# A hybrid mLSTM and DeltaNet block on one core: the DeltaNet output in normal seven-product order throughout, and the mLSTM output's last 512 columns behind it

## The chip, the cores and the metric

The kernel runs on one core of a Trainium2 chip (trn2). The metric is the device time of one execution in microseconds (us). The median of three runs before the change is 2251.95 us (2249.82 to 2252.3).

## The reference

One layer takes x, 512 tokens by 2048 channels, in float32. An input projection feeds two token mixers, an mLSTM and a gated DeltaNet, and two sets of merge gates. Each mixer ends in 512 tokens by 2048 channels, h_a and h_b. What follows is the part that the change touches, cut to its core:

```python
y_a = jnp.matmul(h_a, w_out[:2048])       # mLSTM output, 2048 columns
y_b = jnp.matmul(h_b, w_out[2048:])       # DeltaNet output, 2048 columns
y = sigmoid(gate_a) * y_a + sigmoid(gate_b) * y_b
h = x + y
return h * rsqrt(mean(h * h, axis=-1) + 1e-6) * final_norm_w
```

The last line needs the sum of squares over all 2048 columns of a token before any column of that token can be stored.

## The kernel before, in words

**Number format.** TensorE multiplies float32 by three matmuls of a shorter format: every operand is a high part and a low part, and high times high, high times low and low times high are added in PSUM. A weight tile of 128 by 512 is loaded by the SP queue (L180, L183), ScalarE casts it to the high part `wh` (L136), and VectorE subtracts to get the low part `wl` (L139). The activations are held as `uh` and `ul`, 16 tiles of 128 channels by 512 tokens. All tokens stay on the chip and are cut into four token tiles of 128, so a weight tile of a plain product serves 4 x 3 = 12 matmuls.

**Buffers.** Four buffers of one kind (tag `wr`, NRAW = 4) are shared by the plain weights, by reloaded activations and by gate tiles `ty`; the seven-product part has a second kind (tag `wr3`), three buffers of three tiles.

**Output stage, mLSTM.** The columns 0 to 1023 of y_a are made earlier, in four narrow blocks. At 1965.74 us of the profiled execution two wide blocks begin, columns 1024 to 1535 and 1536 to 2047, each 16 weight tiles x 12 = 192 matmuls (L1570 to L1572). After each, the gate is applied (a tanh form: gate plus one, times the product, times 0.5), x is added, and the result goes to a scratch array in DRAM, `y_d` (L1556 to L1561). During the second wide block `uh` and `ul` are overwritten tile by tile with the DeltaNet's activations (`load_h`), since nothing reads the mLSTM's any more; those stay in DRAM as `hm_d`.

**Output stage, DeltaNet.** y_b is made in two seven-product blocks, as in Strassen's scheme, of 1024 columns each (`OUTS`). A block has an A-half, 8 quads with 4 products of 6 matmuls (192), and a B-half, 8 quads with 3 products (144). A quad is three 128 x 512 tiles of weights loaded into a `wr3` buffer (L533), summed on VectorE (L556, L557) and split. The A-half leaves a sum `ts` in DRAM (`t2o_d`) for the B-half. Gated results of the first block are added into `y_d` by accumulating DMAs of the POOL queue (L1343), each of which holds a `ty` buffer until it has landed.

**The last block before the change** departs from that order. In its A-half POOL subtracts a second weight tile, `b21` (L519 loads it into a `wr` buffer, L560 subtracts, L561 stores to `t2o_d`). Its B-half is `final_y`: 24 single weight tiles (L1401) in the order m5, m7, m1, six matmuls each (L1413 to L1415). Beside it, `hf` (four token tiles of all 2048 columns) is filled from `y_d` (L1435), ScalarE squares (L1431), POOL multiplies by the final norm's weights (`weigh`, L1442), and the factor of a token tile is made at L1447 to L1449. Token tiles 2 and 3 are done ahead of the end; tiles 0 and 1 end behind the last matmuls, and stores go out on SP (L1464).

**What sets the order.** TensorE's instructions stand in the order in which the code is written. On the other engines a scheduler orders by dependence and by priorities (`urgent` ahead, `behind` later). A tick-driven list of generators (`start`, `tick`) sets when loads and side work are issued. `plan`, `limit` and `prepare` say how far ahead plain weights are loaded (4) and split (3). A DMA queue is in order: an issue that waits for a buffer holds up all that stand behind it.

Of the kernel before, what the change touches and what calls it, by code (L numbers as in the profile page):

```python
# [15 lines left out]
P = 128  # L16
# [40 lines left out]
def hybrid_body(  # L57
# [101 lines left out]
    plan += [("o", nb * NO, k) for nb in range(YNARROW * NB // NO, D // NO) for k in range(KT)]  # L159
# [340 lines left out]
    def seven_stage(sbp, su, s4, X, t2_d, w_, k0, blocks, sinks, hook, final=None):  # L500
# [5 lines left out]
                 for g in ("A" if final and b == len(blocks) - 1 else "AB") for i in range(KH)]  # L506
        rawq, partq, b21 = [], {}, {}

        def in_final(b):
            return final is not None and b == len(blocks) - 1  # L510

        def load_b21(q):

            if q < len(quads) and in_final(quads[q][3]):
                _, c1, c2, b, g, i = quads[q]
                k2 = slice((k0 + 2 * i + 1) * P, (k0 + 2 * i + 2) * P)
                with tc.high_priority(offset=2 * PRIO):
                    b21[q] = wp.tile([P, NO], F32, tag="wr", name="b21", bufs=NRAW)
                    nc.sync.dma_start(b21[q], w_[k2, c1:c1 + NO])  # L519
# [25 lines left out]
        def prep_sums(q):  # L545
# [49 lines left out]
        def seven(n0, kind, c1, c2):  # L595
# [5 lines left out]
            if in_final(n0 // (2 * KH)):  # L601
                fin = final(c1, c2, m1, m5, m7, LHS["B"], split, t2_d[(n0 // (2 * KH)) % 2])
# [14 lines left out]
            if in_final(n0 // (2 * KH)):  # L617
                for n in range(KH - 2):
                    prep_sums(n0 + n + 1)
                    prep_pair(n0 + n + 1)  # L620
                    load_quad()
                    for m in range(4):
                        if n == KH - 3 and m == 2:
                            prep_sums(n0 + KH - 1)
                            prep_pair(n0 + KH - 1)
                        product(n, m)
                for m in range(4):
                    for n in (KH - 2, KH - 1):
                        fin(2 * m + n - KH + 2)
                        product(n, m)  # L630
                fin(8)
                return
            N = 2 * KH
            for n in range(N - 2):
                if n == N - 3 and n0 + N + 1 < len(quads) and in_final(quads[n0 + N][3]):
                    load_b21(n0 + N)
# [137 lines left out]
    def begin_mixers():  # L774

        limit[0] = len(plan)
        prepare(nfront - 1)
# [550 lines left out]
    ssf, rf = bia[:, 0:3 * NC].rearrange("p (c n) -> p c n", c=NC), bia[:, 3 * NC:4 * NC]  # L1328

    def sink_y(c1, c2, m1, m5, m7, last):  # L1330

        tgs = {}
        U1, C22 = ([X2[:, q, t, :] for t in range(2)] for q in range(2))

        def load(key, c, col):
            t = tgs[key] = wp.tile([P, NO], F32, tag="wr", name="ty", bufs=NRAW)
            nc.sync.dma_start(t, tg_d[c, :, D + col:D + col + NO])

        def put(key, ps, c, col, now=True):
            t = tgs[key]  # L1340
            with urgent(3) if now else behind("V"):
                V.scalar_tensor_tensor(out=t, in0=t, scalar=1.0, in1=ps, op0=ALU.add, op1=ALU.mult)
            G.dma_start(y_d[c, :, col:col + NO], t, accum_op=ALU.add)  # L1343

        def late_(n, c, col, x_):
            load(n, c, col)
# [3 lines left out]
        def half_b():  # L1350

            for t in range(2):
                load((22, t), 2 + t, c2)
            for t in range(2):
                load((11, t), t, c1)
# [5 lines left out]
            for t in range(2):  # L1361
                load((12, t), t, c2)
# [10 lines left out]
        if not last:  # L1373
            start(half_b(), 4 * KH + 2)
        return (lambda t: put((11, t), m1[t], t, c1)), end5, end7

    def final_y(c1, c2, m1, m5, m7, lhs, split, t4_d):

        U1, C22 = ([X2[:, q, t, :] for t in range(2)] for q in range(2))
        pieces = [(m, i) for m in (1, 2, 0) for i in range(KH)]  # L1380
        ps = (m1, m5, m7)
        rawp, partp = [], []
        hf, fw, jk, ty = {}, {}, {}, {}


        def load_gates():
            order = ((2, c2), (3, c2), (0, c2), (1, c2), (2, c1), (3, c1), (0, c1), (1, c1))
            for n, (c, col) in enumerate(order):
                if n % 3 == 0:
                    t = late["sb"].tile([P, 3, NO], F32, tag="wr3", name="ty", bufs=3)  # L1390
                o = ty[c, col] = t[:, n % 3, :]
                nc.sync.dma_start(o, tg_d[c, :, D + col:D + col + NO])
                yield 1

        def load():
            if len(rawp) < len(pieces):
                m, i = pieces[len(rawp)]
                k2 = slice((KT + 2 * i + 1) * P, (KT + 2 * i + 2) * P)
                with tc.high_priority(offset=2 * PRIO):
                    r = wp.tile([P, 1, NO], F32, tag="wr", name="wr", bufs=NRAW)  # L1400
                    newest["S"] = nc.sync.dma_start(r[:, 0, :], (w_out[k2, c1:c1 + NO], w_out[k2, c2:c2 + NO], t4_d[i])[m]).ins  # L1401
                rawp.append(r)

        def prep():
            if len(partp) < len(pieces):
                with tc.high_priority(offset=2 * PRIO):
                    partp.append(split(rawp[len(partp)], False)[0])

        def part(j, t):
            m, i = pieces[j]  # L1410
            hi, lo = partp[j]
            ah, al = lhs[m](i, slice(t * P, (t + 1) * P))
            T.matmul(ps[m][t], ah, hi, start=False, stop=False, skip_group_check=True)  # L1413
            T.matmul(ps[m][t], ah, lo, start=False, stop=False, skip_group_check=True)  # L1414
            T.matmul(ps[m][t], al, hi, start=False, stop=(i == KH - 1), skip_group_check=True)  # L1415

        def times(c, col, src, tie=True):
            t = ty[c, col]
            with behind("V") if tie else urgent(3):
                V.scalar_tensor_tensor(out=t, in0=t, scalar=1.0, in1=src, op0=ALU.add, op1=ALU.mult)  # L1420

        def plus(c, col, eng, tie=True):
            o = hf[0][:, c, col:col + NO]
            with ExitStack() as e:
                if eng is V:
                    e.enter_context(behind("V") if tie else urgent(3))
                eng.tensor_tensor(out=o, in0=o, in1=ty[c, col], op=ALU.add)  # L1427

        def square(c, a, b, n, tie=True):
            with behind("A") if tie else urgent(3):  # L1430
                A.activation(jk[0][:, 0:b - a], hf[0][:, c, a:b], AF.Square, accum_out=ssf[:, c, n:n + 1])  # L1431

        def known(c, a, b):
            with behind("S"):
                nc.sync.dma_start(hf[0][:, c, a:b], y_d[c, :, a:b])  # L1435

        def weight(a, b):
            with behind("S"):
                nc.sync.dma_start(fw[0][:, a:b], final_norm_w[a:b].partition_broadcast(P))

        def weigh(c, a, b):
            G.tensor_tensor(out=hf[0][:, c, a:b], in0=hf[0][:, c, a:b], in1=fw[0][:, a:b], op=ALU.mult)  # L1442

        def factor(c, tie=True):
            r = rf[:, c:c + 1]
            with behind("V") if tie else urgent(3):
                V.reduce_sum(out=r, in_=ssf[:, c, :], axis=mybir.AxisListType.X)  # L1447
                V.tensor_scalar(out=r, in0=r, scalar1=1.0 / D, scalar2=EPS, op0=ALU.mult, op1=ALU.add)
            G.tensor_tensor(out=r, in0=r, in1=mhalf[:, 0:1], op=ALU.pow)  # L1449

        def by_act(c, a, b, tie=True):
            with behind("A") if tie else urgent(2):
                A.mul(hf[0][:, c, a:b], hf[0][:, c, a:b], rf[:, c:c + 1])

# [171 lines left out]
```

## Time and profile before

| | |
|---|---|
| Runs, median of 3 | 2251.95 us |
| Profiled execution, its own time (span) | 2252.6 us, 0.65 us above the median |
| TensorE busy | 2183.0 us, 97% |
| VectorE busy | 1658.0 us, 74% |
| ScalarE busy | 944.6 us, 42% |
| POOL busy | 294.0 us, 13% |
| Two wide mLSTM blocks | 1965.74 to 2055.50 us |
| First seven-product block | 2055.50 to 2137.23 us |
| Second one: A-half, then final pieces | to 2195.56, to 2241.62 us |
| Behind the last matmul | 10.98 us |

A profile row names a line of the kernel, the engine, the operation, and the output and input tiles. PE is TensorE, DVE VectorE, ACT ScalarE, and SPq the queue of SP. A timeline row begins with start and duration in us, and its bracket says how long the engine had stood idle and what released it.

### The profile page before, as it was taken

To read this page: it belongs to the slowest core of one execution; us is meant where nothing else is said; L and a number is where in the kernel's file an instruction comes from. 1 tells how busy PE (TensorE), PEld (TensorE's weight loads), DVE (VectorE), ACT (ScalarE), POOL (GpSimd) and SP (SyncE) were. 2 spreads that over 40 slices of the span, in tenths; PEclk is the share of its full clock that TensorE was granted. 3 is DMA by queue.
4 is the path that set the end of the run, shared out by engine and by line. 5 is a ranking of instruction groups with operands and counts; after the bars stand their busy time and mean duration, and the time that the engine had idled before them with its cause. 6 is when DMAs were issued, how large, how long until landed. Compare 5 with 4: busy or idle time off the path is not lost. (4 is left out here: it accounts for less than half of the span.)

```text
span 2252.6 us, 33199 instructions
## 1 busy us (share of the span) xinstructions
PE 2183.0 (97%) x11408; PEld 1822.1 (81%) x11408; DVE 1658.0 (74%) x2911; ACT 944.6 (42%) x1824; POOL 294.0 (13%) x362
## 2 busy tenths in 40 slices
PE   7999999999999999998999999999999999999986
PEld 5987888788778778887888888888888899987765
DVE  5787888778877777857786777777767765747777
ACT  4444444445444444433434434343443443323334
POOL 0420000000000000012322131221222110000124
PEclk9999999999999999999999999999999999999988
DMA  5456666567667776767666665757666565958686
GB/s 159 129 166 198 212 202 209 191 194 239 201 202 225 229 222 189 247 195 181 154 162 152 145 167 131 176 136 172 138 167 147 134 172 171 284 155 258 206 238 243
DMA packets 541131, 422.27 MB, mean 187 GB/s; under 512 B 241441, under 2 KB 417794, under 8 KB 540962
## 3 DMA queue, kind: packets, MB, share of 16 engines
q1 hardware_dynamic: 443426, 358.20, 56.7%
q10 hardware_dynamic: 95744, 57.76, 8.4%
q0 software_dynamic: 1792, 4.20, 0.8%
q8 instruction: 89, 1.46, 0.3%
q14 instruction: 80, 0.66, 0.1%
HBM read 335.03 MB, written 85.00 MB: 186 GB/s over the span
## 5 line engine op out<-in xcount | busy, mean ns | idle before, releaser
L136 ACT CAST wh<-wr 128x512 fp32r<-128x512 f32 (+1 forms) x576 | 396.2, 690 | 554.1 <-PE pj L259 275.3
L139 DVE TENSOR_TENSOR wl<-wr,wh 128x512 fp32r<-128x512 f32 (+1 forms) x576 | 479.9, 836 | 178.7 <-ACT wh L136 168.6
L258 PE MATMUL pj<-uh,wh 128*128 128x512 f32 x1024 | 429.9, 420 | 5.5 <-ACT yp L831 5.5
L260 PE MATMUL pj<-uh,wl 128*128 128x512 f32 x1024 | 401.5, 392 | 0.0
L259 PE MATMUL pj<-ul,wh 128*128 128x512 f32 x1024 | 400.5, 391 | 0.0
L611 PE MATMUL ps<-wl,uh 128*128 128x512 f32 x592 | 234.0, 395 | 6.5 <-DVE wl L139 6.4
L610 PE MATMUL ps<-wh,uh 128*128 128x512 f32 x592 | 232.8, 393 | 6.0 <-DVE X L670 5.6
L612 PE MATMUL ps<-wh,ul 128*128 128x512 f32 x592 | 231.1, 390 | 0.0
L260 PEld LDWEIGHTS pj<-uh,wl 128*128 128x128 f32 x1024 | 192.8, 188 | 43.2
L258 PEld LDWEIGHTS pj<-uh,wh 128*128 128x128 f32 x1024 | 193.8, 189 | 40.5 <-ACT yp L831 5.9
L259 PEld LDWEIGHTS pj<-ul,wh 128*128 128x128 f32 x1024 | 194.0, 189 | 33.1
L136 ACT CAST wh<-ts 128x512 fp32r<-128x512 f32 x200 | 123.4, 617 | 222.1 <-DVE ts L568 180.5
L136 ACT CAST wh<-t 128x1024 fp32r<-128x1024 f32 x104 | 109.5, 1053 | 245.1 <-PE ps L612 115.0
L611 PE MATMUL ps<-wl,suh 128*128 128x512 f32 x528 | 205.7, 390 | 0.5 <-DVE wl L139 0.5
L610 PE MATMUL ps<-wh,suh 128*128 128x512 f32 x528 | 205.9, 390 | 0.0
L612 PE MATMUL ps<-wh,sul 128*128 128x512 f32 x528 | 205.5, 389 | 0.0
L139 DVE TENSOR_TENSOR wl<-t,wh 128x1024 fp32r<-128x1024 f32 x104 | 132.0, 1269 | 42.7 <-ACT wh L136 42.0
L139 DVE TENSOR_TENSOR wl<-ts,wh 128x512 fp32r<-128x512 f32 x200 | 139.1, 699 | 31.3 <-ACT wh L136 31.3
L273 PE MATMUL pjt<-wh,uh 128*128 128x256 f32 x512 | 147.6, 288 | 0.8 <-ACT tgs L787 0.7
L275 PE MATMUL pjt<-wl,uh 128*128 128x256 f32 x512 | 144.8, 283 | 0.0
L276 PE MATMUL pjt<-wh,ul 128*128 128x256 f32 x512 | 144.8, 283 | 0.0
L611 PEld LDWEIGHTS ps<-wl,uh 128*128 128x128 f32 x592 | 111.4, 188 | 38.7 <-DVE wl L139 17.0
(321 smaller groups left out, 3845.1 us busy)
## 6 DMA issues: line engine op xcount, KB each, us to landing
wr<-in_w_in_dram SPq DMA_DIRECT2D x680, 256.0 KB, 3.7
wr<-in_w_out_dram SPq DMA_DIRECT2D x144, 256.0 KB, 4.3
t_d<-ts ACTq DMA_DIRECT2D x88, 256.0 KB, 4.3
wr<-t_d SPq DMA_DIRECT2D x88, 256.0 KB, 4.0
wr<-in_w_in_dram SPq DMA_DIRECT2D x96, 128.0 KB, 3.1
xt<-in_x_dram SPq DMA_DIRECT2D x8, 512.0 KB, 8.1
v<-v_d SPq DMA_DIRECT2D x8, 512.0 KB, 6.2
gb<-rows_d SPq DMA_DIRECT2D x16, 256.0 KB, 4.7
```

Of the source, the lines that this page charges most:

```text
L136: newest["A"] = A.copy(hi, src).ins
L139: newest["V"] = V.tensor_tensor(out=lo, in0=src, in1=hi.bitcast(F32), op=ALU.subtract).ins
L258: T.matmul(ps[j], hi[:, k, wsl], uh[:, kt, :], start=(kt == 0), stop=False)
L259: T.matmul(ps[j], hi[:, k, wsl], ul[:, kt, :], start=False, stop=False)
L260: T.matmul(ps[j], lo[:, k, wsl], uh[:, kt, :], start=False, stop=(kt == KT - 1))
L273: T.matmul(o, uh[:, kt, tsl], hi[:, k, :], start=(kt == 0 and c % 2 == 0), stop=False, skip_group_check=True)
L275: T.matmul(o, uh[:, kt, tsl], lo[:, k, :], start=False, stop=False, skip_group_check=True)
L276: T.matmul(o, ul[:, kt, tsl], hi[:, k, :], start=False, stop=(kt == KT - 1), skip_group_check=True)
L610: T.matmul(ps[t], ah, hi, start=(g == "A" and i == 0), stop=False, skip_group_check=True)
L611: T.matmul(ps[t], ah, lo, start=False, stop=False, skip_group_check=True)
L612: T.matmul(ps[t], al, hi, start=False, stop=(i == KH - 1), skip_group_check=True)
```

## The change

Three things change, all in the output stage.

1. **One wide block instead of two** ahead of the DeltaNet: columns 1024 to 1535 only. The DeltaNet's activations replace the mLSTM's during this block.
2. **Both seven-product blocks in normal order.** `b21`, POOL's subtraction and `final_y` are gone. The last block's results do not go to `y_d`: `sink_last` fills `hf` with what is known (from `y_d` for columns up to 1535, from x for the last 512), gates, and adds on POOL (`plus`). From the middle of its B-half on, `load_hm` reads the even tiles of `hm_d` again into `uh` and `ul`.
3. **A new last block**, `last_block`: columns 1536 to 2047 of the mLSTM's output, 192 matmuls, with the channel tiles in the order 0, 2, .. 14, 1, 3, .. 15. The odd tiles of `hm_d` are split beside it. The squares and weighings of the other 1536 columns lie beside it too. The last four weight tiles are run token tile by token tile, and each token tile is ended (`done_c`) when its last matmul is through.

```diff
-    plan += [("o", nb * NO, k) for nb in range(YNARROW * NB // NO, D // NO) for k in range(KT)]
+    plan += [("o", nb * NO, k) for nb in range(YNARROW * NB // NO, D // NO - 1) for k in range(KT)]
+    nlast = len(plan)
+    LAST = [k for o in range(2) for k in range(o, KT, 2)]
+    plan += [("o", D - NO, k) for k in LAST]
...
-                    if in_final(b):
-                        G.tensor_tensor(out=b21[q], in0=b21[q], in1=ts[:, 0, :], op=ALU.subtract)
-                        G.dma_start(t2_d[b % 2, i], b21[q])
-                        load_b21(q + 1)
-                    else:
-                        nc.scalar.dma_start(t2_d[b % 2, i], ts[:, 0, :])
+                    nc.scalar.dma_start(t2_d[b % 2, i], ts[:, 0, :])
...
+    def load_hm(ks, step):
...
+            if k % 2:
...
+                raw = r3[:, n % 3, :]
+            else:
+                raw = wp.tile([P, NO], F32, tag="wr", name="hm", bufs=NRAW)
+            load_tile(raw, hm_d[k])
+            w.append((k, raw))
+            if len(w) > 1:
+                split_hm(*w.pop(0))
+            yield step
...
+        def end1(t):
+            gated(ty[t, c1], m1[t])
+            plus(t, c1, ty[t, c1])
...
+    def hook_y():
+        limit[0] = len(plan)
+        prepare(used[0] - 1)
...
+        def done_c(c):
+            o, r = hf[:, c, nsl], rf[:, c:c + 1]
+            gated(tgs[c], ps[c])
+            with urgent(3):
+                V.scalar_tensor_tensor(out=o, in0=tgs[c], scalar=0.5, in1=o, op0=ALU.mult, op1=ALU.add)
+            square(c, CT, D, 2, False)
+            with urgent(3):
+                V.reduce_sum(out=r, in_=ssf[:, c, :], axis=mybir.AxisListType.X)
+                V.tensor_scalar(out=r, in0=r, scalar1=1.0 / D, scalar2=EPS, op0=ALU.mult, op1=ALU.add)
+            G.tensor_tensor(out=r, in0=r, in1=mhalf[:, 0:1], op=ALU.pow)
+            with urgent(2):
+                A.mul(hf[:, c, 0:HD], hf[:, c, 0:HD], r)
+            nc.sync.dma_start(out[c * P:(c + 1) * P, 0:HD], hf[:, c, 0:HD])
+            with urgent(2):
+                V.scalar_tensor_tensor(out=o, in0=o, scalar=r, in1=fw[:, nsl], op0=ALU.mult, op1=ALU.mult)
+                V.tensor_scalar(out=hf[:, c, HD:CT], in0=hf[:, c, HD:CT], scalar1=r, scalar2=None, op0=ALU.mult)
+            nc.scalar.dma_start(out[c * P:(c + 1) * P, HD:D], hf[:, c, HD:D])
...
+        for kt in ks[:KT - KLAST]:
+            w = next_w("o", CT, kt)
+            for c in range(NC):
+                products(ps, kt, c, *w, ks)
...
+    wide_block(YNARROW * NB // NO)
     for b, blk in enumerate(OUTS):
         seven(2 * KH * b, *blk)
+    last_block()
```

**SP queue, around the end of the first seven-product block.** Before, the gate tile `ty_21012`, which the last results of that block need, stood behind a `b21` load and four quads of the next block (line numbers are those of before):

```order
L519 DMA b21_20982<-in_w_out_dram 128x512
L533 DMA wr3_20994<-in_w_out_dram 128x512 x3
L1337 DMA ty_21004<-tg_d_69 128x512
L533 DMA wr3_21030<-in_w_out_dram 128x512 x3
L533 DMA wr3_21066<-in_w_out_dram 128x512 x3
L533 DMA wr3_21134<-in_w_out_dram 128x512 x3
L1337 DMA ty_21012<-tg_d_69 128x512
```

Now the same two gate tiles, `ty_20686` and `ty_20694`, have no `b21` load ahead of them (line numbers of the changed kernel):

```order
L1302 DMA ty_20686<-tg_d_69 128x512
L524 DMA wr3_20676<-in_w_out_dram 128x512 x3
L1302 DMA ty_20694<-tg_d_69 128x512
L524 DMA wr3_20712<-in_w_out_dram 128x512 x3
L524 DMA wr3_20745<-in_w_out_dram 128x512 x3
```

The second gate tile has moved ahead of three quads. It used to wait until the buffer of `b21_20982` was stored; it now waits for one accumulating DMA of this block.

**SP queue, from the second half of the last B-half into the new block.** Here `hf` loads of 512 KB stand between the last quads, then reloaded `hm` tiles, gate tiles, and the first plain weights `wr`:

```order
L1352 DMA hf_21166<-y_d_17784 128x1024 x4
L524 DMA wr3_21291<-in_w_out_dram 128x512 x2
L524 DMA wr3_21291<-t2o_d_19726 128x512
L1201 DMA hm_21271<-hm_d_68 128x4x128
L1201 DMA hm_21309<-hm_d_68 128x4x128
L524 DMA wr3_21329<-in_w_out_dram 128x512 x2
```

```order
L1201 DMA hm_21349<-hm_d_68 128x4x128
L1201 DMA hm_21385<-hm_d_68 128x4x128
L1201 DMA hm_21417<-hm_d_68 128x4x128
L183 DMA wr_21431<-in_w_out_dram 128x512
L183 DMA wr_21433<-in_w_out_dram 128x512
L183 DMA wr_21435<-in_w_out_dram 128x512
L183 DMA wr_21437<-in_w_out_dram 128x512
L1201 DMA hm_21469<-hm_d_68 128x4x128
L1302 DMA ty_21481<-tg_d_69 128x512
L183 DMA wr_21487<-in_w_out_dram 128x512
```

Six tiles `hm3`, the gate tiles `ty_21345` and `ty_21347`, two 512 KB gate tiles `tga` and two more `hm3` stand between these two pieces. By the waits of the program, `hm_21349` and `hm_21385` wait for POOL's `plus` of the first two gated results, `wr_21431` for the split of `hm_21385`, and each of `wr_21433`, `wr_21435` and `wr_21437` for the `wl` of the weight ahead of it.

**VectorE, the same place.** `ul` splits of `hm` stand ahead of the first weights, and two gatings stand behind the third one:

```order
L1205 SCALAR_TENSOR_TENSOR ul_88<-hm_21349,normc_82,uh_87 128x512
L1205 SCALAR_TENSOR_TENSOR ul_88<-hm_21385,normc_82,uh_87 128x512
L139 TENSOR_TENSOR wl_21440<-wr_21431,wh_21439 128x512
L139 TENSOR_TENSOR wl_21444<-wr_21433,wh_21443 128x512
L139 TENSOR_TENSOR wl_21448<-wr_21435,wh_21447 128x512
L1307 SCALAR_TENSOR_TENSOR ty_21345<-ty_21345,ps_20789 128x512
L1307 SCALAR_TENSOR_TENSOR ty_21347<-ty_21347,ps_20790 128x512
L1205 SCALAR_TENSOR_TENSOR ul_88<-hm_21417,normc_82,uh_87 128x512
L139 TENSOR_TENSOR wl_21490<-wr_21437,wh_21489 128x512
```

Before, this engine had single weight splits of `final_y` here and no `ul` split after the second wide block.

More of the change, by code (lines that the diff above doesn't have):

```diff
@@ L498, in gates, with seven_stage @@
         V.tensor_copy(emcol, pc[:, :, 8:16])
-    def seven_stage(sbp, su, s4, X, t2_d, w_, k0, blocks, sinks, hook, final=None):
+    def seven_stage(sbp, su, s4, X, t2_d, w_, k0, blocks, sinks, hook):
         suh, sul = su
@@ L505, in seven_stage @@
         quads = [(kind, c1, c2, b, g, i) for b, (kind, c1, c2) in enumerate(blocks)
[L506 to L519, printed above, removed]
+                 for g in "AB" for i in range(KH)]
+        rawq, partq = [], {}
         def load_quad():
@@ L1328, in hybrid_body, with y_gate, gated @@
     ssf, rf = bia[:, 0:3 * NC].rearrange("p (c n) -> p c n", c=NC), bia[:, 3 * NC:4 * NC]
+    U1, C22 = ([X2[:, q, t, :] for t in range(2)] for q in range(2))
+    CT = D - NO
+    nsl = slice(CT, D)
+    fin = {}
+    def y_gate(c, col):
+        t = wp.tile([P, NO], F32, tag="wr", name="ty", bufs=NRAW)
+        nc.sync.dma_start(t, tg_d[c, :, D + col:D + col + NO])
+        return t
+    def gated(t, src, now=True):
+        with urgent(3) if now else behind("V"):
+            V.scalar_tensor_tensor(out=t, in0=t, scalar=1.0, in1=src, op0=ALU.add, op1=ALU.mult)
     def sink_y(c1, c2, m1, m5, m7, last):
         tgs = {}
[L1333 to L1337, printed above, removed]
         def put(key, ps, c, col, now=True):
[L1340 to L1343, printed above, removed]
+            gated(tgs[key], ps, now)
+            G.dma_start(y_d[c, :, col:col + NO], tgs[key], accum_op=ALU.add)
         def late_(n, c, col, x_):
-            load(n, c, col)
+            tgs[n] = y_gate(c, col)
             yield 6
@@ L1371, in end5 @@
             put((12, t), m5[t], t, c2)
-        if not last:
-            start(half_b(), 4 * KH + 2)
+        if last:
+            return sink_last(c1, c2, m1, m5, m7)
+        start(half_b(), 4 * KH + 2)
         return (lambda t: put((11, t), m1[t], t, c1)), end5, end7
[L1377 to L1388, printed above, removed]
-                if n % 3 == 0:
[L1390 to L1453, printed above, removed]
-        def by_dve(c, a, b, tie=True, weighed=False):
-            o, r = hf[0][:, c, a:b], rf[:, c:c + 1]
-            with behind("V") if tie else urgent(2):
-                if weighed:
-                    V.tensor_scalar(out=o, in0=o, scalar1=r, scalar2=None, op0=ALU.mult)
-                else:
-                    V.scalar_tensor_tensor(out=o, in0=o, scalar=r, in1=fw[0][:, a:b], op0=ALU.mult, op1=ALU.mult)
-        def store(c, a, b):
-            nc.sync.dma_start(out[c * P:(c + 1) * P, a:b], hf[0][:, c, a:b])
-        def open_hf():
@@ L1536, in final_y @@
[L1536 to L1545 removed]
+            for n, shape in (("hf", [P, NC, D]), ("fw", [P, D]), ("jk", [P, HD])):
+                fin[n] = pool.tile(shape, F32, tag=n, name=n)
```

236 lines of the change are left out of this document (125 added, 111 removed).

## The prediction

> **What bounds the kernel now.** I read the page first, then the busy time of each engine by stage, then TensorE's waits stage by stage, then what SP's queue waits for, and last single rows of the timeline.
>
> ```profile
> span 2252.6 us, 33199 instructions
> PE 2183.0 (97%) x11408; PEld 1822.1 (81%) x11408; DVE 1658.0 (74%) x2911; ACT 944.6 (42%) x1824; POOL 294.0 (13%) x362
> ```
>
> TensorE is busy 97% of the span, so the kernel is bound by matmuls nearly everywhere. The profiled execution took 2252.6 us, 0.65 us above the median of the runs; I sum against its span and take 0.65 off at the end. The change touches only what begins at 1965.74 us. The next view cuts that stretch into two wide blocks, first seven-product block, A-half of the second, its final pieces, and what lies behind the last matmul.
>
> ```profile
> core 0: us, PE busy (x) PEld busy (x) DVE busy (x) ACT busy (x) POOL busy (x), PEclk, DMA share, GB/s
> 1965.74:2055.50 89.76, 88.23 (x386) 71.93 (x385) 45.24 (x70) 29.20 (x48) 0.00 (x0) 1.00 0.62 191
> 2055.50:2137.23 81.73, 78.47 (x337) 62.46 (x336) 63.70 (x83) 31.40 (x45) 6.05 (x6) 1.00 0.72 225
> 2137.23:2195.56 58.33, 49.77 (x193) 39.12 (x192) 45.27 (x51) 18.19 (x27) 17.32 (x19) 0.88 0.83 241
> 2195.56:2241.62 46.06, 38.61 (x145) 29.01 (x143) 36.66 (x42) 23.18 (x44) 22.22 (x12) 0.89 0.70 248
> 2241.62:2252.60 10.98, 0.00 (x0) 0.00 (x0) 4.03 (x10) 3.02 (x4) 1.27 (x2) 0.73 0.50 205
> 2197.00:2224.00 27.00, 24.19 (x104) 18.84 (x102) 21.76 (x24) 15.07 (x29) 14.90 (x8) 1.00 0.94 328
> ```
>
> The unit for all that follows is the distance of matmuls at full clock, from two rows of the second wide block that stand 48 matmuls apart:
>
> ```profile
> 2009.29 0.39 PE L1570 MATMUL py<-wh,uh 128*128 128x512 f32 x1
> ...
> 2020.17 0.39 PE L1570 MATMUL py<-wh,uh 128*128 128x512 f32 x1
> ```
>
> 10.88 us over 48 is 0.227 us. So 192 matmuls are 43.5 us, 144 are 32.6 us, and the 12 of one weight tile are 2.72 us. Against that, the A-half of the second seven-product block loses 14.8 us (58.33 - 43.5) and the final pieces lose 13.5 us (46.06 - 32.6), at a granted clock of 0.88 and 0.89. The first seven-product block loses 5.5 us (81.73 - 76.2) at a clock of 1.00. The waits say where. First those of the first block, then those of the second:
>
> ```profile
> PE ps L611 <- DVE wl L139: 2.0, 3, 0.9
> PE ps L610 <- DVE X L670: 1.1, 1, 1.1
> ```
>
> ```profile
> PE ps L1414 <- DVE wl L139: 6.1, 4, 2.0
> PE ps L610 <- DVE ty L1342: 5.1, 1, 5.1
> PE ps L610 <- ACT wh L136: 2.0, 1, 2.0
> ```
>
> In the second block a single wait of 5.1 us for a gating (L1342) stands out, and four waits for split weights in the final pieces. SP's queue shows what holds that gating up, and the timeline what follows it:
>
> ```profile
> SPq L519 <- DMA y_d<-ty: 7.6, 4, 3.9
> ```
>
> ```profile
> 2142.07 4.16 SPq L519 DMA_DIRECT2D b<-in_w_out_dram  x3
> ```
>
> ```profile
> 2145.94 0.80 PE L610 MATMUL ps<-wh,tuh 128*128 128x512 f32 x1 [5.15 <-DVE ty L1342]
> 2146.54 0.63 PE L611 MATMUL ps<-wl,tuh 128*128 128x512 f32 x1
> 2146.97 0.63 PE L612 MATMUL ps<-wh,tul 128*128 128x512 f32 x1
> ```
>
> The gate tile shares its four buffers with `b21`, and the queue stands 7.6 us in issues of `b21` that wait for accumulating stores. Behind the 5.15 us gap the matmuls stand 0.43 us apart: half clock.
>
> **The change part by part.**
>
> *Wide blocks, 89.76 to 46.2, so -43.5.* One of the two 192-matmul blocks leaves this place. The 2.7 us beyond 87 (89.76 - 2 x 43.5) come where the DeltaNet's activations replace the mLSTM's, and that now happens in the remaining block; I keep them.
>
> *First seven-product block, 0.* Its code is the same.
>
> *Second block's A-half, 58.33 to 44.9, so -13.4.* `b21` goes: eight loads, eight subtractions on POOL and eight stores. The gate tile that was late stands ahead of three quads now. What is late next is SP's wait for accumulating stores ahead of the fifth quad, but that quad is due some 20 us into the half, and the stores begin within 2 us of its start. I leave 1.4 us of stalls, half of what the first block's waits sum to. Bounds: 43.5 (none) and 58.33 (the wait only changes its cause).
>
> *Final pieces become a normal B-half, 46.06 to 35.1, so -11.0.* 32.6 us of matmuls and 2.5 us of stalls, as the first block loses beyond its A-half. Beside it SP loads `hf`, the norm's weights and the reloaded tiles. Counted in the order: 3 MB behind the A-half's last matmul, then quads, 2 MB more of `hf`, and tiles, together 12.75 MiB, 13.4 MB, until the first weight of the last block. With the queue full, DMA moved 328 GB/s (last row of the table by stage), so this takes 40.8 us. That is the cover which the next term lacks.
>
> *Entry to the last block, +10.4.* This wait is new. Let T0 be the A-half's last matmul. Two paths lead to the first split weight. By volume: T0 + 40.8, then landing of the weight and its split. By dependence: the first pair of results ends with 20 of the 24 products, T0 + 27.2 + 2.5; two gatings and two additions on POOL follow before `hm_21349` and `hm_21385` may load; they land, are split, and only then SP may issue `wr_21431`, which stands behind them with every later weight. The prices:
>
> ```profile
> wr<-in_w_out_dram SPq DMA_DIRECT2D x1, 256.0 KB, 2.9
> ```
>
> ```profile
> wr<-in_w_out_dram SPq DMA_DIRECT2D x6, 256.0 KB, 5.7
> ```
>
> ```profile
> 2197.12 0.62 ACT L136 CAST wh<-wr 128x512 fp32r<-128x512 f32 x1 [6.05 <-PE ps L1415]
> ...
> 2197.78 0.69 DVE L139 TENSOR_TENSOR wl<-wr,wh 128x512 fp32r<-128x512 f32 x1 [1.33 <-ACT wh L136]
> ```
>
> ```profile
> L1427 POOL TENSOR_TENSOR hf<-hf,ty 128x512 f32<-128x512 f32 x4 | 6.4, 1601 | 26.0 <-DVE ty L1420 26.0
> L1442 POOL TENSOR_TENSOR hf<-hf,fw 128x1024 f32<-128x1024 f32 (+1 forms) x6 | 14.3, 2414 | 0.6 <-ACT jkf L1431 0.6
> ```
>
> The first is a landing, issue to end, at 2225 us in the final pieces (I take 3.0), the second the median at 2132 to 2146 us with many transfers under way. So: 29.7, gating 0.7, two additions 3.2, landing 3.0, two splits behind one another about 2.4 (1.36 and most of a second), landing 3.0, split 1.4: T0 + 43.4. The volume gives nearly the same, 40.8 + 0.8 + 1.4 = T0 + 43.0. Where both press, each lengthens the other: with both landings at 5.7 the chain ends at T0 + 48.8. I take T0 + 45.5, nearer to the short landings, since the volume is just done when they start. TensorE is ready at T0 + 35.1, so the wait is 10.4 us (8 to 14).
>
> *The last block, 43.5 + 15.4 = 58.9, so +58.9.* The first seven weights come one by one, since each waits for the `wl` of the one ahead: landing 3.0, cast and subtraction 1.36 (2197.12 to 2197.78 and 0.69), issue 0.1, so 4.45 us against 2.72 us of matmuls: seven gaps of 1.73 are 12.1 us. Then gate tiles free the other buffers, and weights run two us apart. For half clock I add 1.3. These rows show why:
>
> ```profile
> 2225.27 0.50 PE L1414 MATMUL ps<-wl,uh 128*128 128x512 f32 x1 [1.80 <-DVE wl L139]
> ...
> 2226.82 0.63 PE L1413 MATMUL ps<-wh,uh 128*128 128x512 f32 x1
> 2227.25 0.63 PE L1414 MATMUL ps<-wl,uh 128*128 128x512 f32 x1
> ```
>
> After a 1.80 us gap (and two of 1.1 ahead of it) matmuls go to a distance of 0.43, so a weight tile takes 5.1 us, longer than the 4.45 to the next weight; one tile after the entry and one more, at 0.65 each, is 1.3. The bounds are 0 and seven times 0.65, 4.6. The Trainium skill (TensorE: Matmul & The Clock Gate, Part 1, the HAM clock gate) has the clock fall after an idle window of about 3.4 us. The row of 1.80 us does not agree; the row of 5.15 us does. By the rule the gaps of 1.73 us would cost nothing, and the sum would be 0.65 lower.
>
> Then POOL's weighings:
>
> ```profile
> 2226.34 0.68 DVE L139 TENSOR_TENSOR wl<-wr,wh 128x512 fp32r<-128x512 f32 x1
> ...
> 2232.60 2.78 DVE L139 TENSOR_TENSOR wl<-wr,wh 128x512 fp32r<-128x512 f32 x1
> ```
>
> The same subtraction takes 0.68 alone and 2.78 beside a weighing. The 5120 columns of weighing before took 14.3 us, so 6144 take 17.2 us. In the order they stand at the sixth to thirteenth weight, about 2.15 a weight, beside 1.4 of VectorE's own: 3.5 against 2.72. At most 0.8 x 7, 5.6 us; at least nothing, if the splits run ahead. I take 2.0, because half of these weights come while TensorE waits for loads anyway. The sixteen reloaded tiles add 0.62 us each on ScalarE and 0.69 on VectorE, 11 us there; half of it lies beside the B-half, where VectorE had 9.4 us free (46.06 - 36.66) and loses the waits for POOL's work, and half is in the 1.4 a weight. Their 4 MiB of transfers are in the 13.4 MB, and the eight loads and eight stores of `b21` go.
>
> *Behind the last matmul, 10.98 to 12.3, so +1.3.* Four token tiles end 2.72 us apart, and VectorE takes their steps in turn; before, tiles 0 and 1 did.
>
> ```profile
> 2245.63 0.75 DVE L1461 SCALAR_TENSOR_TENSOR hf<-hf,bia,fw 128x512 f32<-128x512 f32 x1 [0.44 <-POOL bia L1449]
> 2246.30 0.48 DVE L1459 TENSOR_SCALAR hf<-hf,bia 128x512 f32<-128x512 f32 x1
> ```
>
> The chain of the last tile is the same in kind: gating, addition, square, factor, closing product, store; half of the eight stores move from SP's queue to ScalarE's. In the order, two closing operations of the third tile (0.75 + 0.48) stand between the fourth one's gating and its addition: 1.2, rounded up.
>
> *Sum.* -43.5 - 13.4 - 11.0 + 10.4 + 58.9 + 1.3 = +2.7. The span becomes 2255.3, a run 2254.6 us: 0.12% above the median. About 0.2%, 4.5 us, is what a measurement of this kernel can tell from no change, so this forecast is no change.
>
> **The rivals.**
>
> *Slower: the DMA queue backs up at the entry.* Place: the loads from T0 to the first weights, 13.4 MB in the order. It decides when those loads land later than about 4 us instead of 3. For it: 5.7 us in the busy stretch, and a DMA share of 0.94 when the queue is full. Against it: the bulk is due at T0 + 40.8, before the chained loads start. Price: 3.3 at the entry (to 48.8) and up to 0.5 for each of the seven weights, a fifth of the way to 5.7: 2258 to 2261.
>
> *Slower: the A-half's wait stays with another cause.* The queue still waits for accumulating stores there, and half clock follows. Price 5.15 and 3: 2263. Here the change doesn't do what it says.
>
> *Faster: only the lower bounds hold.* Entry at T0 + 43.2, no half clock, no weighing in the way: -2.3 - 1.3 - 2.0 gives 2249.
>
> *Faster: the last block isn't starved.* The waits that I read for the first weights are there in the program, but if gatings and additions are early, two buffers alternate and a weight comes every 2.3 us. This takes 12.1 and 1.3 away: 2241. With the lower bounds of entry and weighing as well: 2237. Against it: the program lists four weights behind one another.
>
> **How the numbers follow.** Chances: forecast as summed, 2249 to 2260, 0.45 (of it 0.32 within 0.2% and 0.13 slower); queue backed up 0.20; A-half's wait stays 0.07; lower bounds 0.10 (0.06 within 0.2%, 0.04 faster); not starved 0.10; not starved and early 0.08. Faster by over 0.2%: 0.22, within: 0.38, slower: 0.40. The time is that of the likeliest, 2254.6, whose own range is 2249 to 2260. The range for 8 in 10, 2241 to 2266, leaves out the early case and the end of both slow ones.
>
> **What would show it.** In the changed profile: the A-half without a wait over 2 us and at a clock near 1.00; the B-half at about 35 us; one wait of 8 to 14 us ahead of the last block, released by a split weight; then about seven waits of 1.7 us for `wl`; subtractions of 2 us and more beside POOL's weighings; 12 us behind the last matmul. The forecast is wrong if SP doesn't hold the first weights back, or if it holds quads of the B-half back too.

## The result, and the profile after

The changed kernel takes 2254.65 us, the median of 20 runs (2249.87 to 2263.48), beside 2250.49 us for the kernel before (20 runs, 2245.18 to 2257.95). The ratio is 1.0022, with a 95% interval of 1.0013 to 1.0031: slower, by about as much as can be told from no change. The forecast was 2254.6 us.

The agreement is better than the terms deserve, and its closeness is luck: the kernel before is 1.5 us faster in these 20 runs than in the three that the forecast started from, and errors of the terms cancel. In the profiled execution the first wide block begins at 1958.03 us, 7.7 us earlier than in that of before, although every engine has the same instructions in the same order up to there. So the two spans (2252.8 and 2252.6 us) say nothing of the change; the stretch behind that point does. It is 294.8 us long now, against 286.9 before and 289.6 in the forecast. This is its busy time by stage (one wide block, first seven-product block, A-half and B-half of the second, the entry to the last block, the last block, and the end):

```profile
core 0: us, PE busy (x) PEld busy (x) DVE busy (x) ACT busy (x) POOL busy (x), PEclk, DMA share, GB/s
1958.03:2005.62 47.59, 45.87 (x195) 36.94 (x193) 33.16 (x53) 21.05 (x36) 0.00 (x0) 0.96 0.74 223
2005.62:2084.63 79.01, 77.45 (x337) 62.83 (x337) 60.27 (x78) 29.99 (x42) 3.66 (x4) 1.00 0.70 220
2084.63:2131.91 47.28, 45.47 (x193) 37.09 (x192) 37.38 (x48) 18.06 (x26) 3.45 (x4) 0.96 0.86 246
2131.91:2168.94 37.03, 34.43 (x145) 26.37 (x143) 24.01 (x33) 12.17 (x15) 5.31 (x4) 1.00 0.99 335
2168.94:2179.76 10.82, 0.17 (x2) 0.01 (x1) 2.40 (x5) 2.06 (x3) 0.00 (x0) 0.72 0.55 168
2179.76:2241.32 61.56, 51.49 (x192) 37.37 (x192) 39.06 (x46) 26.80 (x51) 25.75 (x14) 0.94 0.31 103
2241.32:2252.80 11.48, 0.15 (x1) 0.00 (x0) 4.74 (x11) 3.98 (x5) 1.27 (x2) 0.68 0.67 274
```

What the old order lost in the second seven-product block is gone: its two halves take 84.3 us instead of 104.4. The rows of the entry and of the last block take it back. For 10.8 us TensorE has nothing to do, and the 192 matmuls behind that need 61.6 us instead of 43.5. TensorE's waits over this whole stretch show where:

```profile
PE py L1447 <- ACT wh L136: 17.0, 7, 10.7
PE ps L595 <- DVE wl L139: 5.4, 6, 1.8
PE py L1448 <- DVE wl L139: 5.3, 9, 2.7
```

The seven waits for `wh` are the entry (10.7), five of about 1 us in the last block and one in the wide block; the nine for `wl` hold one of 2.7. Rows of TensorE's timeline show how regular they are (the first matmul of weights 1, 3, 4, 5, 6 and 7, and the long wait inside the eighth):

```profile
2179.76 0.79 PE L1447 MATMUL py<-wh,uh 128*128 128x512 f32 x1 [10.65 <-ACT wh L136]
...
2188.67 0.49 PE L1447 MATMUL py<-wh,uh 128*128 128x512 f32 x1 [0.91 <-ACT wh L136]
2193.09 0.50 PE L1447 MATMUL py<-wh,uh 128*128 128x512 f32 x1 [0.87 <-ACT wh L136]
2197.94 0.50 PE L1447 MATMUL py<-wh,uh 128*128 128x512 f32 x1 [1.32 <-ACT wh L136]
2202.45 0.50 PE L1447 MATMUL py<-wh,uh 128*128 128x512 f32 x1 [1.01 <-ACT wh L136]
2206.92 0.51 PE L1447 MATMUL py<-wh,uh 128*128 128x512 f32 x1 [0.96 <-ACT wh L136]
2213.39 0.50 PE L1448 MATMUL py<-wl,uh 128*128 128x512 f32 x1 [2.72 <-DVE wl L139]
```

They stand 4.4 to 4.9 us apart, where full speed is 2.72. SP's queue shows why: the issues of the first four weights are one row of its timeline, and it is 13.91 us long.

```profile
2175.78 13.91 SPq L183 DMA_DIRECT2D wr<-in_w_out_dram  x4
```

What the queue waited for between 2174 and 2192 us: each of the last three of these issues waits for the landing of the weight ahead (up to 2.9 us) and then for its subtraction (up to 1.4 us).

```profile
SPq L183 <- DMA wr<-in_w_out_dram: 8.2, 3, 2.9
SPq L183 <- DVE wl L139: 4.2, 3, 1.4
```

The eighth weight is another matter. VectorE's and POOL's rows there:

```profile
2210.49 2.85 DVE L139 TENSOR_TENSOR wl<-wr,wh 128x512 fp32r<-128x512 f32 x1
2213.26 1.78 DVE L1205 SCALAR_TENSOR_TENSOR ul<-hm,normc,uh 128x512 fp32r<-128x512 f32 x1
2214.96 2.87 DVE L139 TENSOR_TENSOR wl<-wr,wh 128x512 fp32r<-128x512 f32 x1
```

```profile
2209.98 9.00 POOL L1363 TENSOR_TENSOR hf<-hf,fw 128x1024 f32<-128x1024 f32 x4
```

Four weighings fill POOL for 9.00 us, and a subtraction that takes 0.68 us alone takes 2.85 beside them.

### The profile page after: what moved, and what is told of

Read it like the earlier page. It is cut to its first block, busy times and chain, and to the rows that moved or that the text cites. A ratio compares the mean times of both kernels' runs of the same rounds, so it can differ in the third digit from the quotient of the medians.

```text
span 2252.8 us, 33173 instructions
## 1 busy us (share of the span) xinstructions
PE 2181.4 (97%) x11408; PEld 1821.3 (81%) x11408; DVE 1664.2 (74%) x2925; ACT 954.1 (42%) x1832; POOL 283.7 (13%) x352
## 4 chain that ended last, share of the span: by engine, by line
PE 64%; DMA 14%; DVE 10%; issue 6%; SPq 2%; ACT 2%; POOL 1%; ACTq 0%; DVEq 0%; POOLq 0%
PE pj L261 10%; PE pj L263 10%; PE pj L262 10%; PE ps L595 9%; PE ps L594 9%; PE ps L596 9%; DVE wl L139 4%; DMA wr<-t_d 4%; DMA wr<-in_w_in_dram 2%; DMA wr<-in_w_out_dram 2%; SPq L524 1%; ACT wh L136 1%; DMA wr<-t2o_d 1%; DMA hr<-hm_d 1%; DVE t L547 1%
## 5 line engine op out<-in xcount | busy, mean ns | idle before, releaser
L136 ACT CAST wh<-wr 128x512 fp32r<-128x512 f32 (+1 forms) x560 | 390.0, 698 | 558.3 <-PE pj L262 280.0
L139 DVE TENSOR_TENSOR wl<-wr,wh 128x512 fp32r<-128x512 f32 (+1 forms) x560 | 469.7, 842 | 179.9 <-ACT wh L136 172.2
L595 PE MATMUL ps<-wl,uh 128*128 128x512 f32 x624 | 246.4, 395 | 6.8 <-DVE wl L139 6.7
L594 PE MATMUL ps<-wh,uh 128*128 128x512 f32 x624 | 245.0, 393 | 3.8 <-DVE X L636 2.9
L596 PE MATMUL ps<-wh,ul 128*128 128x512 f32 x624 | 243.4, 390 | 0.0
L136 ACT CAST wh<-ts 128x512 fp32r<-128x512 f32 x208 | 128.4, 617 | 223.9 <-DVE ts L554 169.8
L139 DVE TENSOR_TENSOR wl<-t,wh 128x1024 fp32r<-128x1024 f32 x104 | 127.2, 1223 | 49.1 <-ACT wh L136 48.5
L595 PEld LDWEIGHTS ps<-wl,uh 128*128 128x128 f32 x624 | 117.4, 188 | 40.8 <-DVE wl L139 17.8
L594 PEld LDWEIGHTS ps<-wh,uh 128*128 128x128 f32 x624 | 117.4, 188 | 34.2 <-DVE X L636 8.7
```

Of the source, the lines that this page charges most:

```text
L136: newest["A"] = A.copy(hi, src).ins
L139: newest["V"] = V.tensor_tensor(out=lo, in0=src, in1=hi.bitcast(F32), op=ALU.subtract).ins
L594: T.matmul(ps[t], ah, hi, start=(g == "A" and i == 0), stop=False, skip_group_check=True)
L595: T.matmul(ps[t], ah, lo, start=False, stop=False, skip_group_check=True)
L596: T.matmul(ps[t], al, hi, start=False, stop=(i == KH - 1), skip_group_check=True)
```

## The experiments

My theory had three parts: one shared buffer hands the first weights on one by one; a chain of POOL's additions and two landings makes the entry; POOL's weighing adds a little. The rivals were the DMA volume, for entry and rate, and the weighing as the main cause. Each experiment, four to ten runs, was timed against runs of the kernel before that were made with it (medians 2248.87 to 2250.79 us). To compare it with the changed kernel I set the ratios side by side, and I read the stages in its profile. The stages in us, from first matmul to first matmul; the last two columns are the weights 1 to 7 and 8 to 13 of the last block:

| kernel | run, ratio to before | A-half | B-half | entry | last block | 1-7 | 8-13 |
|---|---|---|---|---|---|---|---|
| before | 2250.49 | 58.3 | | | | | |
| changed | 2254.65, 1.0022 | 47.3 | 37.0 | 10.8 | 61.6 | 30.5 | 22.8 |
| early gating | 2245.15, 0.9979 | 44.5 | 35.9 | 7.0 | 54.5 | 22.1 | 24.3 |
| own buffers | 2245.77, 0.9974 | 45.0 | 37.7 | 6.7 | 54.3 | 21.5 | 24.7 |
| no weighing | 2251.51, 0.9992 | 45.6 | 35.8 | 9.2 | 55.5 | 30.1 | 17.2 |
| both | 2242.06, 0.9959 | 46.7 | 36.7 | 6.7 | 48.8 | 21.8 | 18.9 |
| early gating, no weighing | 2237.93, 0.9946 | 45.7 | 36.9 | 7.4 | 47.2 | 21.8 | 17.2 |
| 3 MiB deferred | 2239.88, 0.9957 | 44.3 | 36.4 | 2.2 | 53.2 | 21.3 | 23.8 |
| 5 MiB deferred | 2236.83, 0.9947 | 48.0 | 33.7 | 1.2 | 53.1 | 23.8 | 21.2 |
| before, b21 apart | 2246.73, 0.9987 | 52.2 | | | | | |

(At full speed seven weights are 19.0 us, six are 16.3.)

### Early gating

```diff
         def end5(t):
             add(m5[t], U1[t], m5[t])
-            gated(ty[t, c2], m5[t], False)
+            gated(ty[t, c2], m5[t])
```

> One word changes in the changed kernel: the gating of the m5 results runs as soon as its input is there, instead of late. Two of the four shared buffers come free about 20 us earlier, so the reloaded tiles and the first weights of the last block wait for POOL's additions only, and three weights can be under way. Theory (the first weights come one by one because one shared buffer serves them): the entry wait falls from 10.7 to about 6 us, the last block from 61.6 to about 52 us, the run from 2254.7 to about 2241 us. Rival (the DMA volume ahead of the first weights sets their rate): entry wait stays over 9 us, weights stay 4.4 us apart, run within 2251 to 2257. Rival (POOL's weighing blocks VectorE and sets the block's length): entry shorter, last block still about 58, run about 2247.

Measured: 2245.15 us (2241.58 to 2250.66), ratio 0.9979 (0.9961 to 0.9997). The entry fell to 7.0 and the first seven weights to 22.1 us, nearly full speed behind the first: with the same loads in the same order, so the volume doesn't set their rate. The block came to 54.5 and not to 52, and the run to 2245 and not to 2241, since the weights 8 to 11 now take 5.3, 4.5, 4.5 and 4.5 us: for these the second rival was right. VectorE's rows there show the same two durations again and again:

```profile
2195.82 2.86 DVE L139 TENSOR_TENSOR wl<-wr,wh 128x512 fp32r<-128x512 f32 x1
2198.60 1.77 DVE L1205 SCALAR_TENSOR_TENSOR ul<-hm,normc,uh 128x512 fp32r<-128x512 f32 x1
2200.30 2.88 DVE L139 TENSOR_TENSOR wl<-wr,wh 128x512 fp32r<-128x512 f32 x1
2203.10 1.78 DVE L1205 SCALAR_TENSOR_TENSOR ul<-hm,normc,uh 128x512 fp32r<-128x512 f32 x1
2204.80 2.86 DVE L139 TENSOR_TENSOR wl<-wr,wh 128x512 fp32r<-128x512 f32 x1
```

2195.82 to 2200.30 is 4.48 us: one subtraction, one `ul` split, each waiting for a weighing. It is nearly the 4.45 us of a landing and a split, a different cause with the same period.

### Own buffers for the reloaded tiles

```diff
-                raw = wp.tile([P, NO], F32, tag="wr", name="hm", bufs=NRAW)
+                raw = fin["pool"].tile([P, NO], F32, tag="hm", name="hm", bufs=2)
```

> In the changed kernel the eight even reloaded tiles get two buffers of their own, in room that the last block's pool has left; the shared ones go to weights and gate tiles. Then the first weight waits for POOL's first addition only, and two buffers alternate for the weights. Theory (shared buffer): entry wait 2 to 4 us instead of 10.7, a weight every 2.3 us, so TensorE's 2.72 us a weight bind; last block 45 to 53 us; run about 2236. Rival (DMA volume): the first weight still lands 8 us or more behind the B-half, or the B-half itself grows by what the entry loses; run within 2250 to 2257.

Measured: 2245.77 us (2240.25 to 2248.8), ratio 0.9974 (0.9955 to 0.9993). The first seven weights run at 21.5 us, as the theory had it. The entry is 6.7 and not 2 to 4, and the run lies between the theory's 2236 and the rival's 2250 to 2257: at the entry the rival fits better. The edit also reorders some loads of the queue (reloaded tiles come earlier, one `hf` load and the norm's weights later); that was not tried apart. The windows of B-half and entry (columns as above):

```profile
2135.00:2172.67 37.67, 34.22 (x145) 26.45 (x143) 27.18 (x35) 13.36 (x17) 6.23 (x4) 1.00 1.00 346
2172.67:2179.36 6.69, 0.16 (x2) 0.00 (x1) 0.90 (x3) 0.62 (x1) 0.00 (x0) 0.72 0.88 286
```

The DMA share is 1.00 through the B-half and 0.88 in the entry; in the changed kernel's entry it was 0.55.

### No weighing

The eight multiplications of `weigh` are left out, so the first 1536 columns lack the final norm's weights.

```diff
     def weigh(c, a, b):
-        G.tensor_tensor(out=fin["hf"][:, c, a:b], in0=fin["hf"][:, c, a:b], in1=fin["fw"][:, a:b], op=ALU.mult)
+        pass
```

> The changed kernel without POOL's eight multiplications by the final norm's weights, so the first 1536 columns are stored without that factor. Theory (price 2 us, bounds 0 to 5.6): the entry stays 10.7, the first seven weights stay 4.4 us apart, and the subtractions beside POOL fall from 2.8 to 0.7 us; last block 57 to 59 instead of 61.6; run 2250 to 2253. Rival (the weighing sets the whole second part of the block): last block 55 or less, run about 2247.

Measured: 2251.51 us (2248.26 to 2256.52), ratio 0.9992 (0.9981 to 1.0004). The first seven weights take 30.1 us, as before the edit: their 4.45 us have nothing to do with POOL's weighing. The block loses 6.1 us, not 2.6 to 4.6, and 5.6 of them in the weights 8 to 13; at 55.5 it lies below the theory's 57 to 59 and just above the rival's 55, while the run lies in the theory's range. The entry came to 9.2 instead of 10.7; why was not tried.

```profile
PE py L1447 <- ACT wh L136: 13.6, 6, 9.0
PE py L1448 <- DVE wl L139: 1.9, 7, 0.6
```

TensorE's waits in that run: the entry of 9.0, five for `wh`, and no wait for `wl` over 0.6 where there had been one of 2.7.

### Both, and early gating without weighing

The fourth kernel has the first two edits together.

> Early gating and own buffers for the reloaded tiles together: four shared buffers for weights and gate tiles. Theory (shared buffer): entry as with own buffers, 2 to 4 us, and no starved weight; last block 45 to 50 us, held only by POOL's weighing; run 2230 to 2236. Rival (DMA volume): no better than either alone; run over 2245.

Measured: 2242.06 us (2239.58 to 2246.7), ratio 0.9959 (0.9943 to 0.9974). The block is 48.8, as expected: two weights beside the weighings are slow, the rest runs at 2.72 behind a first one at half clock. Entry and run are not what I expected, 6.7 and 2242 instead of 2 to 4 and at most 2236. Its DMA stayed full in both stretches:

```profile
2134.00:2170.60 36.60, 33.91 (x145) 26.50 (x143) 27.66 (x35) 13.36 (x17) 6.40 (x5) 1.00 1.03 361
2170.60:2177.30 6.70, 0.20 (x2) 0.04 (x1) 2.30 (x5) 0.69 (x2) 2.37 (x2) 0.88 1.01 327
```

To tell the two periods of 4.5 us apart, one kernel joined early gating with `weigh` left out:

> Early gating as in the first run, and POOL's eight multiplications by the final norm's weights left out, so the first 1536 columns are stored without that factor. In the run with early gating alone the first seven weights went at 2.7 us and four later ones at 4.5 us each, beside POOL's weighings. Theory (those four are held by VectorE, which takes turns with POOL's weighings): they go to 2.7 us too and the block from 54.5 to 46 to 48 us. Rival (a second stretch in which weights share a buffer, with landing and split of 4.45 us): the four stay at 4.4 to 4.5 us and the block over 52 us.

Measured: 2237.93 us (2236.76 to 2239.95), ratio 0.9946 (0.993 to 0.9962). The weights 8 to 13 take 17.2 us instead of 24.3, the block 47.2: as the theory said. TensorE's waits in that block come to two rows, the entry and next to nothing:

```profile
PE py L1447 <- ACT wh L136: 7.3, 1, 7.3
PE py L1448 <- DVE wl L139: 0.8, 2, 0.6
```

### Loads deferred

Both edits, and loads that are needed late are queued behind the newest plain weight: the odd `hm3` tiles and `tga` (3 MiB), and in one of the two kernels also the first 1024 columns of `hf` (5 MiB).

```diff
-                nc.sync.dma_start(raw, src.rearrange("(k p) n -> p k n", p=P))
+                newest["S"] = nc.sync.dma_start(raw, src.rearrange("(k p) n -> p k n", p=P)).ins
...
+            if k % 2:
+                with behind("S"):
+                    load_tile(raw, hm_d[k])
+            else:
+                load_tile(raw, hm_d[k])
...
+            with behind("S"):
+                for c in range(2):
+                    known(c, 0, HD)
```

> Early gating and own buffers as in the run with both, and 5 MiB of loads that nothing needs before the last block's second half (the eight odd reloaded tiles, the two 512 KB gate tiles, and the first 1024 columns of hf) are queued behind the last block's fourth weight. Theory (with the buffers free, the entry is held by the DMA volume ahead of the first weight, 361 GB/s at a full queue): entry wait from 6.7 to 2 to 3 us, B-half 34 to 36 us, no half clock at the first weight, run about 2234 to 2237. Rival (the entry is held by the chain of gating, addition, landing and split): entry stays over 5 us and the run at about 2242. Rival (the loads that were moved now starve the block itself): entry short, but waits of 2 us and more at the fifth to ninth weight; run about 2242.

> As the run that defers 5 MiB, but the first 1024 columns of hf stay where they were, so 3 MiB move. Theory (volume): entry wait between the two, 2 to 4 us, run 2235 to 2239. Rival (chain): as the run with both, 2242.

Measured: 2236.83 us (2234.78 to 2241.24), ratio 0.9947 (0.9929 to 0.9964) with 5 MiB, and 2239.88 us (2239.4 to 2241.2), ratio 0.9957 (0.994 to 0.9973) with 3 MiB. The entry falls to 1.2 and 2.2 us; with 5 MiB the B-half is down to 33.7:

```profile
2133.29:2167.02 33.73, 33.28 (x145) 26.67 (x143) 26.53 (x36) 13.20 (x17) 6.50 (x5) 1.00 0.79 273
2167.02:2168.23 1.21, 0.15 (x1) 0.00 (x0) 0.90 (x3) 0.62 (x1) 1.21 (x2) 1.00 0.55 191
2168.23:2221.34 53.11, 47.75 (x192) 37.27 (x192) 40.21 (x44) 27.02 (x51) 21.30 (x13) 0.94 0.63 208
```

So the volume held the entry once the buffers were free. But the last block grew from 48.8 to 53.1 and 53.2, which gives back about half of what entry and B-half gained with 5 MiB and nearly all of it with 3 MiB. The intervals of both ratios overlap that of the kernel with both edits (0.9943 to 0.9974), so the runs don't tell these kernels apart, and the one with 3 MiB missed its 2235 to 2239.

With 5 MiB the second rival was right in part: besides the entry there are waits of 0.74 and 2.08 us for `wh`, at the sixth and the eighth weight, and two loads that were issued at 2174.78 and 2176.58 us took 7.8 and 8.0 us to land. The waits for `wl` are 2.5 us. With 3 MiB it was not starvation. There TensorE has one long wait behind the entry, 4.59 us for the `wl` of the eighth weight, and VectorE's rows ahead of it are these:

```profile
2190.90 2.90 DVE L1307 SCALAR_TENSOR_TENSOR ty<-ty,X 128x512 f32<-128x512 f32 x1
2193.72 4.12 DVE L1205 SCALAR_TENSOR_TENSOR ul<-hm,normc,uh 128x512 fp32r<-128x512 f32 x3
2197.77 2.83 DVE L139 TENSOR_TENSOR wl<-wr,wh 128x512 fp32r<-128x512 f32 x1
```

The subtraction stands behind a late gating and three `ul` splits, and from 2190.62 us on POOL's weighings lie beside them: VectorE and POOL take turns once more. That the deferral moved these splits there is argued, not tried. The kernel with 5 MiB deferred has the lowest median of those in the study that leave nothing out.

### The kernel before, with b21 in other buffers

```diff
-                    b21[q] = wp.tile([P, NO], F32, tag="wr", name="b21", bufs=NRAW)
+                    b21[q] = wp.tile([P, NO], F32, tag="tg", name="b21", bufs=3)
```

> The kernel before with one edit: the b21 tiles take the three buffers of the sums instead of the four shared with the gate tiles. POOL subtracts and stores as before. Theory (sharing buffers with the gate tiles holds up the gating at L1342 and brings the 5.1 us wait and the half clock behind it): the second block's A-half falls from 58.3 to 46 to 50 us, the wait of 5.1 us goes, run 2241 to 2246. Rival (POOL's subtractions and their stores slow VectorE and SP's queue): A-half stays over 55 us, or the wait moves to the sums, run 2249 or slower.

Measured: 2246.73 us (2243.74 to 2249.93), ratio 0.9987 (0.9977 to 0.9996). TensorE's waits in its A-half:

```profile
PE ps L611 <- DVE wl L139: 2.5, 2, 1.9
PE ps L610 <- ACT wh L136: 2.2, 1, 2.2
PE ps L610 <- DVE ty L1342: 0.4, 1, 0.4
```

The wait for the gating went from 5.1 to 0.4 us, and the A-half from 58.3 to 52.2. That is 6.1 of the 11.0 us which the change took out of this half, between the two expectations (46 to 50, or over 55): waits of 4.7 us for `wl` and `wh` stay. Whether POOL's subtractions or the loads and stores of `b21` cause those was not tried.

## Why the prediction held, term by term

*Wide block, 46.2 forecast, 47.6 measured.* It lost 4.1 us, not 2.7: two waits of 1.24 and 0.38 us near its end, and half clock behind them. *First seven-product block, 81.7 and 79.0.* I put no change here. But in the changed kernel and in all seven of the study with the normal order behind it, it takes 77.4 to 80.2 us, and in the two with `b21` 81.7 and 82.4. The first `b21` load falls into its end; that this is the cause was not tried.

*A-half, 44.9 and 47.3.* The 5.15 us wait is gone, and the experiment on the kernel before shows that the shared buffers made it. One wait of 1.8 us and a clock of 0.96 remain; the other kernels with the normal order lie between 44.3 and 48.0.

*B-half, 35.1 and 37.0.* I counted 40.8 us of transfers as cover for the entry and did not charge them to this half. The queue was at 0.99 with 335 GB/s; with 5 MiB deferred the half took 33.7.

*Entry, 10.4 and 10.8.* The mechanism is the chain as it was laid out; that the size agrees is luck, since errors cancel. The gating of the first pair began at 2164.36 us, 32.5 behind T0 instead of 29.7, and the additions ended at 2167.66. The two tiles took 7.1 and 6.5 us to land (median 6.8 in the row below), more than the long price of 5.7. They were split at 2175.76, and the weight, issued at 2175.78, took 3.3, near the short price. The first matmul came at T0 + 47.9 instead of 45.5, but the B-half had ended 1.9 us late too. That the volume stood right behind the chain was said in the working; the runs with free buffers showed it.

```profile
hm<-hm_d SPq DMA_DIRECT2D x2, 256.0 KB, 6.8
```

*Last block, 58.9 and 61.6.* The starvation was right in mechanism and size: the first seven weights lost 11.5 us against 12.1 and 0.65 for one at half clock. The sign that I named for it, about seven waits of 1.7 us for `wl`, did not come: five of 0.9 to 1.3 us for `wh` stand in its place. The eighth to thirteenth lost 6.5 us against 2.0 and another 0.65. **The step that failed is the price of the weighing**: "I take 2.0, because half of these weights come while TensorE waits for loads anyway." The weighings did not begin while TensorE was starved. They stand on POOL behind its last addition, which ended at 2210.02 us, just when the starved stretch was over, and without them the block is 6.1 us shorter, 5.6 of it in these six weights: my upper bound, where the sum had 2.0.

*Half clock.* It stood where I put one of the two: 0.58 in the first 4.96 us, behind the entry. Between 2184.72 and 2210.29 us, with its waits of about 1 us, the clock was 1.00. By the rule that the forecast cited from the Trainium skill (TensorE: Matmul & The Clock Gate, Part 1) such gaps cost nothing, and in this stretch the trace agrees. Elsewhere it does not: matmuls went to a distance of 0.43 us behind the waits of 1.24 and 0.38 us in the wide block, behind the 1.81 us in the A-half, and behind the 2.72 us at 2213.39 (from 2214.65 on), all less than the 3.4 us of that page. What tells these cases apart was not tried. The rows of the wide block:

```profile
1998.22 0.50 PE L1447 MATMUL py<-wh,uh 128*128 128x512 f32 x1 [1.24 <-ACT wh L136]
...
2000.53 0.63 PE L1449 MATMUL py<-wh,ul 128*128 128x512 f32 x1
2000.96 0.63 PE L1447 MATMUL py<-wh,uh 128*128 128x512 f32 x1
```

*End, 12.3 and 11.5.* Two closing operations of the third tile (L1540, L1541) stand between the fourth one's gating and its addition, where the order has them, and one of the second tile ahead of that gating:

```profile
2241.87 0.48 DVE L1541 TENSOR_SCALAR hf<-hf,bia 128x512 f32<-128x512 f32 x1
2242.26 0.68 DVE L1307 SCALAR_TENSOR_TENSOR tga<-tga,py 128x512 f32<-128x512 f32 x1
2242.86 0.75 DVE L1540 SCALAR_TENSOR_TENSOR hf<-hf,bia,fw 128x512 f32<-128x512 f32 x1
2243.52 0.48 DVE L1541 TENSOR_SCALAR hf<-hf,bia 128x512 f32<-128x512 f32 x1
2243.91 0.68 DVE L1530 SCALAR_TENSOR_TENSOR hf<-tga,hf 128x512 f32<-128x512 f32 x1
```

VectorE ends 6.3 us behind the last matmul, 1.1 us later than before; behind that the stores take 5.2 us instead of 5.8, which I had not counted.

The sum of the stages missed by 5.2 us (294.8 against 289.6) while the run met its forecast to 0.05 us. The measured difference of the medians, 4.2 us, lies between that of the sum (2.7) and that of the two profiled stretches (7.9).

As for the rivals: "the DMA queue backs up at the entry" came true for the two reloaded tiles, which landed in 7.1 and 6.5 us: 6.6 us lie between the last addition and the second landing, where the chain had 3.0. It did not for the first four weights, which landed in 3.0 to 3.3 us. The volume was also the next bound behind the one that the change has. "The last block isn't starved" is what one word in the code brings about: early gating.

## What to carry to other kernels

When work is moved to the end of a kernel, count which buffers its first loads may use and who still holds them: here a gating with low priority kept two of four buffers for 20 us, and making it urgent was worth 0.43% (ratios 1.0022 and 0.9979). Two stretches with the same period can have different causes, so take each away by itself. A cover can be spent twice: the transfers that hide behind one stage lengthen it, and bind the next as soon as its first bound is gone.

## What the runs showed of the hardware

With the queues full this core moved 335 to 361 GB/s (DMA share 0.99 to 1.03), and a 256 KB load, 2.9 us in a quieter stretch, took 6.5 us there (the median of twelve reloaded tiles in the changed kernel):

```profile
hm<-hm_d SPq DMA_DIRECT2D x12, 256.0 KB, 6.5
```

In these runs VectorE's subtractions and `ul` splits, which have two operands in SBUF, and POOL's multiplications take strict turns: 2.86 and 1.77 us, instead of 0.68 and 0.74, follow one another as long as POOL has work. The Trainium skill (SBUF — State Buffer, Who interferes with whom) says that a VectorE instruction with two SBUF inputs contends with a GpSimd (POOL) instruction that reads SBUF, and that what they share is an exclusive lock; the trace agrees. And identical instructions reached the first wide block between 1957.66 and 1966.12 us in the profiled executions of this study, a spread of 8.5 us, which is more than the change was worth.
